# Reciprocals before the broadcast in a two-layer hybrid attention kernel, and the gates' products in smaller portions

## The chip, the core and the metric

The kernel runs on one core of a Trainium2 chip. The core has five engines that run side by side, each through its own instruction stream in order: TensorE (PE in the profile, its weight loads PEld), VectorE (DVE), ScalarE (ACT), GpSimd (POOL) and SyncE (SP), whose stream issues most of the DMAs. They wait for one another by semaphores. The metric is device time in microseconds (us), the median of several executions; less is better.

## What is computed

Two layers of a diffusion trunk over 512 latent tokens and 256 context tokens of width 1024. Each layer normalises its input, projects it once, runs two attention branches over parts of that projection, multiplies each by a SiLU gate, projects them to the model width, merges them by sigmoid gates, projects once more and adds the result, scaled by a residual gate, to the stream. The residual gate is a part of `silu(c) @ w_ada + b_ada`. The second branch is grouped-query attention:

```python
def _attend(q, k, v):
    s = jnp.einsum('bqkgd,btkd->bkgqt', q, k).astype(jnp.float32) * (HEAD_DIM ** -0.5)
    p = jax.nn.softmax(s, axis=-1).astype(v.dtype)
    return jnp.einsum('bkgqt,btkd->bqkgd', p, v)
...
    b_att = _gqa_latent(qb, k_all, v_all)          # 8 query heads, 2 key heads, 768 keys
...
    o_a = (a_att * jax.nn.silu(a_z)) @ w_o_a
    o_b = (b_att * jax.nn.silu(b_z)) @ w_o_b
    merged = jax.nn.sigmoid(g_a) * o_a + jax.nn.sigmoid(g_b) * o_b
    return merged @ w_out
...
    x_new = x + gate_x * out_x
```

In the first layer the context tokens are updated as well, so that they too have queries; in the second they are not.

## The kernel before

**Numbers in two halves.** Large products are made of three matmuls (`mm3`, L421): high half by high half, high by low, low by high. A weight tile of 128x512 comes by an SP DMA into `raw`, ScalarE writes its rounded high half `whi`, and VectorE or GpSimd the rest, `wlo` (`load_w` L385, `load_w2` L400).

**Order.** A planner walks through the program as it is written, with its own costs of each instruction, and places each on its engine's stream when it holds that the inputs are there. What it has placed is fixed: on the chip each engine takes its stream in order. The helper `behind(engine, fn)` (L461) ties what `fn` issues on one engine behind the instruction issued last on that engine. Transposes that are put off (`turn_late`, L473) are tied in this way on TensorE.

**Before grouped-query attention (the projection stage).** In layer 0 the list `bg` (L1085) holds the residual gates' products, 34 steps from `gate_steps((0, 1), ...)`: for each of two halves of the inner dimension one load of the vector `cb` (two DMAs), and then, for 8 tiles and 2 vectors each, one product with its sum over the free dimension (`dot`, L280): L285 on VectorE, tied behind the latest VectorE instruction. The first of the two products of a tile issues the tile's load (`rawb`, L278, on SP); two buffers hold the tiles. In layer 1 `bg` is empty. Six projections of keys and values (`tok_proj`, L1097) run two steps each; then the loop over `qt` token blocks (six in layer 0) makes the queries: a projection of 24 matmuls of 128x512, the squares (ScalarE), their sums (L493, VectorE), the power -0.5 (L496, GpSimd), the scaling (L505) and the rotation (L574, and for latent blocks L576 on GpSimd and L579), all of which end in four transposes (L517) that are put off by two blocks; and then `run(bg, 4)` (L1114) takes four steps from the list. So the 22 steps that are left are all issued by the sixth block. After that come four pieces of filling work (`fill`, L1122; two in layer 1), each a projection of the merge gates, with the transposes that are still put off. Then the pool of this stage is closed (L1125), and the pool of the attention takes over its memory, tile by tile.

**Grouped-query attention.** It runs through 8 units `u` (`pipeline`, L1004): a pair of heads and half of the latent queries each. `gq_first` (L1137) makes four score tiles of 128x768 (L879, L880), a bound of their maximum (L1151, VectorE), the exponentials with their sums over the keys (L1152, ScalarE, sums into `r`, 128x2x2, one column for each of two query blocks and two heads), and two halves in 16 bits (L824 on ScalarE, L825 on VectorE or GpSimd), which a DMA transposes. `gq_second` (L1166) of the unit before follows, and then filling work. In `gq_second` the sums are not divided into the probabilities but into the gate: `divide` (L831) makes reciprocals, each repeated 64 times, as a tile `rb` of 128x256; two transposes on TensorE (L836) turn it into one half of a PSUM tile, and VectorE multiplies it and a factor `back` into the gate (L837). `pair_values` (L839) then multiplies the turned probabilities with the values into the other half of that PSUM tile (L844), and L1179 multiplies both. Layer 0 has a second `divide` for the context queries in every second unit, with the sums `rc`; that makes 8 + 4 divisions in layer 0 and 8 in layer 1.

**Filling work there.** The rest of the merge gates' projections (L612, L616) and the first branch's output projection (high and low halves of its input L658 and L659, products L694), by `run(fill, ...)` after each unit; before the last unit's values, `early` (L1181) issues loads and high and low halves of the second branch's gate.

Of the kernel before, what the change touches and what calls it, by code (L numbers as in the profile page):

```python
# [60 lines left out]
def hybrid_kernel(es: ExitStack, tc, x, ctx, cvec, w_ada, w_ada0, small, gvec, w_in, w_o_a, w_o_b, w_out,  # L61
                  bias_int, bias_edge, rope, ident_d, out):
    nc = tc.nc
    V, S, G, T = nc.vector, nc.scalar, nc.gpsimd, nc.tensor
# [10 lines left out]
    def nm(s):  # L75
        uid[0] += 1
        return f"{s}_{uid[0]}"
# [188 lines left out]
    def ada_steps(l, tiles, halves, nv, pool, queue=None):  # L266

        cb = {}

        def load(h):  # L270
            cb[h] = pool.tile([128, 2, 512], F32, tag="cb", name=nm("cb"), bufs=1)
            for v in range(nv):
                src = cd[8 * v + 4 * h:8 * v + 4 * h + 4].rearrange("k p -> (k p)").unsqueeze(0)
                nc.sync.dma_start(cb[h][:, v, :], src.to_broadcast([128, 512]))

        def load_tile(h, i):
            cb["w"] = pool.tile([128, 512], F32, tag="rawb", name=nm("rawb"), bufs=2)
            (queue or nc.sync).dma_start(cb["w"], w_ada[l, h, i])  # L278

        def dot(h, i, v):  # L280
            if v == 0:
                load_tile(h, i)
            w = cb["w"]
            o = w if v == nv - 1 else pool.tile([128, 512], BF16, tag="junk", name=nm("junk"), bufs=1)
            behind(ON_DVE, lambda: V.tensor_tensor_reduce(o, w, cb[h][:, v, :], 1.0, 0.0, ALU.mult, ALU.add,  # L285
                                                          asum[:, i, h, v:v + 1]))
        res = []
        for h in halves:
            res += [lambda h=h: load(h)] + [lambda h=h, i=i, v=v: dot(h, i, v) for i in tiles for v in range(nv)]
        return res  # L290
# [6 lines left out]
    def ada_mod(l):  # L297
        mod_finish(l, ada_sum(0, 16, 2).rearrange("p (a k) v -> p a k v", a=2), 0, 8)

    def ada_gate(l, nv, pool):  # L300

        g = sp.tile([128, 2, 8], F32, tag="ag", name=nm("ag"), bufs=1)
        n = 8 * nv
        V.tensor_tensor(g[:, 0:nv], ada_sum(16, 24, nv)[:, :, 0:nv].rearrange("p k v -> p v k"),
                        gcol[:, 52 + 8 * l:60 + 8 * l].unsqueeze(1).to_broadcast([128, nv, 8]), ALU.add)
        V.tensor_scalar(g[:, 0:nv], g[:, 0:nv], 0.5, None, ALU.mult)
        pt = psw(512, "t")
        T.transpose(pt[0:n, 0:128], g[:, 0:nv].rearrange("p v k -> p (v k)"), ident)
        gt = pool.tile([16, 128], F32, tag="agt", name=nm("agt"), bufs=1)
        S.copy(gt[0:n], pt[0:n, 0:128])  # L310
        nc.sync.dma_start(gd[l][0:n], gt[0:n])
# [121 lines left out]
    def tok_proj(w, n, a, t, evac):  # L433

        ps = psw(n)
        tok_mm(ps, w, n, a, t, 0, KT)
        evac(t, ps)
        turn_late(hp["lag"])
# [22 lines left out]
    def behind(engine, fn, after=None):  # L461

        n = len(nc.cur_bb.bb.instructions)
        after = latest(engine, 1) if after is None else after
        fn()
        for i in nc.cur_bb.bb.instructions[n:]:
            if i.engine == engine:
                for last in after:
                    tc.add_manual_dep(i, last, mybir.DependencyInfo(
                        mybir.DependencyClass.NoSync, mybir.DependencyReason.DATA), reason="program order")  # L470
                after = [i.name]

    def turn_late(n):  # L473

        while len(hp["late"]) > n:
            behind(ON_PE, hp["late"].pop(0))

    def run(fill, n):
        for _ in range(min(n, len(fill))):
            fill.pop(0)()  # L480
# [102 lines left out]
    def layer(l, hx, nxt, start):  # L583
# [8 lines left out]
        def gate_steps(halves, pool):  # L592
            return ada_steps(l, range(16, 24), halves, nv, pool)
# [104 lines left out]
        if first:  # L698
# [22 lines left out]
            bg = ada_steps(1, range(16), (0,), 2, hp["p"])  # L721
        else:
# [5 lines left out]
            bg = gate_steps((0, 1), hp["p"]) + [lambda: ada_gate(l, nv, hp["p"])]  # L728
# [49 lines left out]
        if True:  # L778
# [52 lines left out]
            def divide(ps, r, dst, back):  # L831

                rb = att["p"].tile([128, 2, 128], F32, tag="rb", name=nm("rb"), bufs=2)
                V.reciprocal(rb.rearrange("p i (e d) -> p i e d", e=2), r.unsqueeze(3).to_broadcast([128, 2, 2, 64]))
                for i in range(2):
                    T.transpose(ps[:, 128 * i:128 * i + 128], rb[:, i, :], ident)  # L836
                V.scalar_tensor_tensor(dst, ps, back, dst, ALU.mult, ALU.mult)  # L837
# [21 lines left out]
            def stage_k(src, e, kh, kl, dup):  # L859

                k = rows(src, e)
                V.tensor_copy(rows(kh, e), k)
                S.copy(rows(kh, 1 - e), k)
                (G if dup else V).tensor_tensor(rows(kl, e), k, F(rows(kh, e)), ALU.subtract)
                if dup:
                    S.copy(rows(kl, 1 - e), F(rows(kl, e)))
# [56 lines left out]
            def open_att(name, width, n_p, n_t, n_h):  # L923
                st = ExitStack()
                att["p"] = st.enter_context(tc.tile_pool(name=name, bufs=2, reuse_waits="tile"))
                att["w"], att["np"], att["nt"], att["nh"] = width, n_p, n_t, n_h
                att["turn"], att["spare"] = 0, False
                return st
# [150 lines left out]
            def split_vb():  # L1079
                size(vf.rearrange("p t n -> p (t n)"), vbig[:, 1152:1920], vbig[:, 2946:2947])  # L1080
                shrink(vbig[:, 2946:2947], vs, vbig[0:1, 2948:2949], 0.5)
                halves(vf.rearrange("p t (h d) -> p (t h) d", h=2), vb.rearrange("p t h q d -> p (t h) q d"),
                       vs[:, 0:1])

            bg = gate_steps((0, 1), hp["p"]) if first else []  # L1085
# [25 lines left out]
                    rope_heads(4, ps, rs, gbc[:, 0, :], None, qbv, t)  # L1111
            for t in range(qt):
                tok_proj(w_q, 512, a_hx, t, evac_bq)
                run(bg, 4)  # L1114
                if t == STAGE_T[0]:
                    split_vb()
                if t in STAGE_T:
                    e = STAGE_T.index(t)
                    stage_k(kbv[:, 0, :], e, gkt[e][0], gkt[e][1], True)

            zb = big("zb")
            for i in range(PRE_GQ * len(spans)):  # L1122
                run(fill, 1)
                turn_late(1 if i == 0 else 0)
            bp_es.close()  # L1125
            gq_es = open_att(f"gq{l}", 768, NP_GQ[l], 0, NH_GQ[l])
            open_ps(s=(2, 1024), v=(1, 512))
# [38 lines left out]
            def gq_second(u, st):  # L1166

                j, b = u // 2, u % 2
                ht, r, cts, rcs = st
                vsl = lambda k, q: vb[:, k, j // 2, q, :]  # L1170
                ps = psw(512, "t")
                work = [(ps, zv[:, j, 256 * b:256 * b + 256], r, vsl, lambda e, a, k: ht[:, :, e, 6 * a + k, :], 6)]
                if b == 1 and first:
                    work.append((psw(512, "v"), zv[:, j, 512:768], rcs, lambda k, q: vsl(4 + k, q),
                                 lambda e, a, k: cts[e][:, a, :, k, :], 2))
                for ps, dst, r, v, pr, n in work:
                    divide(ps[:, 256:512], r, dst, vs[:, 1:2])
                    behind(ON_PE, lambda: pair_values(ps[:, 0:256], v, pr, n), [])
                    V.tensor_tensor(dst, ps[:, 0:256], dst, ALU.mult)  # L1179
# [11 lines left out]
        with tc.tile_pool(name=f"mrg{l}", bufs=1, reuse_waits="tile") as mp:  # L1191
# [34 lines left out]
            bg = ada_steps(1, range(16), (1,), 2, mp, G) + [lambda: ada_mod(1)] if first else []  # L1226
# [205 lines left out]
    def nxt():  # L1432
        if not hx1:
            hx1.extend([[big("hx") for _ in range(2)] for _ in range(2)])
        return hx1
    layer(0, hx0, nxt, start)
    layer(1, hx1, None, None)


# [73 lines left out]
```

## Time and profile before

| what | value |
|---|---|
| median of 3 runs | 1114.02 us (1111.32 to 1115.77) |
| the profiled execution's own time | 1115.85 us |
| its span, first to last instruction | 1114.1 us |
| VectorE busy over the span | 783.1 us |
| ScalarE busy over the span | 607.9 us |
| GpSimd busy over the span | 441.2 us |

The profile is of one execution. Its views group instructions by line and shape, say who waited for whom, list the instructions of an engine in order of time, and sum up the busy time of each engine in a stretch. Matmuls are pipelined, so that TensorE can be busy without being at its peak; the ends of matmuls are modelled. A line of a view names the engine, the line of the kernel, the operation and its output and inputs.

### The profile page before, as it was taken

Reading aid. Unit: us, or ns where it says so; the run is one execution under the profiler, and the core shown is the slowest. Engines: PE = TensorE matmul, PEld = TensorE weight load, DVE = VectorE, ACT = ScalarE, POOL = GpSimd, SP = SyncE. Lnnn points to the kernel's source line nnn. Section 1 sums busy time; section 2 is a strip of 40 time slices with the busy share of each in tenths; the row PEclk is TensorE's granted clock in tenths of the full one; section 3 lists DMA queues with packets and bytes.
Section 4 is the critical chain, followed back from the end, with each engine's and each line's share of the span. In section 5 each row is a group of like instructions: output and inputs, shape, how many; then the busy total and the mean of one; then the engine's idle time right before and its main releaser. Section 6 shows DMA issues by size and latency. Waiting matters only on the chain. (4 is left out here: it accounts for less than half of the span.)

```text
span 1114.1 us, 17673 instructions
## 1 busy us (share of the span) xinstructions
PE 1074.7 (96%) x6032; PEld 883.2 (79%) x6032; DVE 783.1 (70%) x1626; ACT 607.9 (55%) x1236; POOL 441.2 (40%) x375
## 2 busy tenths in 40 slices
PE   8999999899999899988999999999999999999998
PEld 5688888788887778876888778888877888877777
DVE  4667799974388486766576875466997665879573
ACT  6464279776333467665231275444999346676430
POOL 1054235554256143353412444332455472453531
PEclk9999999999999999999999999999999999999999
DMA  9455325555545277789624532453555536889742
GB/s 369 149 169 149 90 70 116 124 137 121 174 121 179 86 177 185 174 219 248 210 76 130 189 120 69 136 170 102 126 145 126 150 113 171 195 236 218 201 151 77
DMA packets 236002, 171.83 MB, mean 154 GB/s; under 512 B 160140, under 2 KB 201864, under 8 KB 234248
## 3 DMA queue, kind: packets, MB, share of 16 engines
q1 hardware_dynamic: 228576, 156.31, 51.6%
q0 software_dynamic: 2368, 7.87, 2.1%
q10 hardware_dynamic: 4968, 6.53, 1.8%
q8 instruction: 47, 0.77, 0.3%
q14 instruction: 43, 0.35, 0.1%
HBM read 115.58 MB, written 17.32 MB: 119 GB/s over the span
## 5 line engine op out<-in xcount | busy, mean ns | idle before, releaser
L825 POOL TENSOR_TENSOR h<-p,h 128x256 f16<-128x256 f32 (+2 forms) x104 | 111.2, 1078 | 199.5 <-ACT h L824 154.2
L410 POOL TENSOR_TENSOR wlo<-raw,whi 128x512 fp32r<-128x512 f32 x70 | 97.7, 1399 | 136.8 <-ACT whi L408 100.5
L423 PE MATMUL psf<-hx,whi 128*128 128x512 f32 (+1 forms) x360 | 137.3, 382 | 1.5 <-DVE zt L614 1.2
L424 PE MATMUL psf<-hx,whi 128*128 128x512 f32 (+1 forms) x360 | 135.7, 377 | 0.0
L425 PE MATMUL psf<-hx,wlo 128*128 128x512 f32 (+1 forms) x360 | 135.3, 376 | 0.0
L408 ACT CAST whi<-raw 128x512 fp32r<-128x512 f32 x136 | 82.9, 620 | 74.0 <-DMA raw<-in_w_in_dram 52.5
L423 PE MATMUL psx<-whi,hx 128*128 128x512 f32 (+1 forms) x328 | 121.7, 373 | 0.0
L424 PE MATMUL psx<-wlo,hx 128*128 128x512 f32 (+1 forms) x328 | 120.1, 367 | 1.3 <-DVE wlo L396 1.3
L425 PE MATMUL psx<-whi,hx 128*128 128x512 f32 (+1 forms) x328 | 120.1, 367 | 0.0
L396 POOL TENSOR_TENSOR wlo<-raw,whi 128x512 fp32r<-128x512 f32 x40 | 59.2, 1483 | 126.5 <-ACT whi L393 83.1
L393 ACT CAST whi<-raw 128x512 fp32r<-128x512 f32 x88 | 54.0, 624 | 94.3 <-PE psx L425 32.1
L496 POOL TENSOR_TENSOR ss<-ss,ehalf 128x8 f32<-128x8 f32 (+2 forms) x40 | 63.6, 1594 | 78.0 <-DVE ss L493 69.6
L824 ACT CAST h<-p 128x256 f16<-128x256 f32 (+2 forms) x136 | 81.2, 617 | 12.3 <-DMA ht<-h 9.3
L1151 DVE CUSTOM_DVE_ANT_0 p<-pss,vb 128x768 f32<-128x768 f32 x64 | 59.9, 949 | 35.1 <-PE pss L880 31.2
L1152 ACT ACTIVATE p<-pss,mx 128x768 f32<-128x768 f32 x64 | 57.5, 901 | 41.0 <-DVE mx L1151 40.6
L423 PEld LDWEIGHTS psf<-hx,whi 128*128 128x128 f32 x360 | 67.8, 188 | 14.7 <-DVE zt L614 1.6
L410 DVE TENSOR_TENSOR wlo<-raw,whi 128x512 fp32r<-128x512 f32 x66 | 60.8, 925 | 26.3 <-ACT whi L408 26.2
L425 PEld LDWEIGHTS psf<-hx,wlo 128*128 128x128 f32 x360 | 67.8, 188 | 11.7
L424 PEld LDWEIGHTS psf<-hx,whi 128*128 128x128 f32 x360 | 67.9, 189 | 11.2 <-issue 0.6
L424 PEld LDWEIGHTS psx<-wlo,hx 128*128 128x128 f32 x328 | 62.0, 189 | 11.6 <-DVE wlo L396 2.4
L425 PEld LDWEIGHTS psx<-whi,hx 128*128 128x128 f32 x328 | 61.9, 189 | 10.5 <-DVE hx L339 0.4
L423 PEld LDWEIGHTS psx<-whi,hx 128*128 128x128 f32 x328 | 61.9, 189 | 9.4 <-issue 0.2
(330 smaller groups left out, 2938.9 us busy)
## 6 DMA issues: line engine op xcount, KB each, us to landing
raw<-in_w_in_dram SPq DMA_DIRECT2D x168, 256.0 KB, 3.0
rawb<-in_w_ada_dram SPq DMA_DIRECT2D x48, 256.0 KB, 2.7
raw<-in_w_out_dram SPq DMA_DIRECT2D x32, 256.0 KB, 2.9
tg<-gs SPq DMA_DIRECT2D x4, 1536.0 KB, 8.4
rawx<-in_w_ada_dram SPq DMA_DIRECT2D x4, 1024.0 KB, 10.2
rawy<-in_w_ada_dram SPq DMA_DIRECT2D x4, 1024.0 KB, 9.9
gs<-zt ACTq DMA_DIRECT2D x16, 256.0 KB, 2.6
raw<-in_w_o_a_dram SPq DMA_DIRECT2D x16, 256.0 KB, 3.7
```

Source lines behind the costliest of these rows:

```text
L393: S.copy(hi[:, :n], raw[:, :n])
L396: e.tensor_tensor(lo[:, :n], raw[:, :n], F(hi[:, :n]), ALU.subtract)
L408: S.copy(hi, raw)
L410: lo_eng(i).tensor_tensor(lo, raw, F(hi), ALU.subtract)
L423: T.matmul(ps, lhs[0], rhs[0], start=first, stop=False)
L424: T.matmul(ps, lhs[0], rhs[1], start=False, stop=False)
L425: T.matmul(ps, lhs[1], rhs[0], start=False, stop=last)
L496: G.tensor_tensor(ss, ss, ehalf[:, :n], ALU.pow)
L824: S.copy(h[:, 0], p[:, :n])
L825: eng.tensor_tensor(h[:, 1], p[:, :n], h[:, 0], ALU.subtract)
L1151: V.tensor_tensor_reduce(p, pss, lift, -1.0, 3e38, ALU.add, ALU.min, mx[:, 0:1])
L1152: S.activation(p, pss, AF.Exp, bias=mx[:, 0:1], accum_out=r[:, i, e:e + 1])
```

## The change

The reciprocal is taken of the sums themselves, in place (128x4), by VectorE; ScalarE then writes each of them 64 times side by side into `rb`. And in the projection stage each block of the query loop takes three steps from `bg`, not four; each of the pieces of filling work after the loop takes one; and whatever is left then is taken before the pool is closed (in layer 0 nothing is: 12 + 18 + 4 = 34).

```diff
             def divide(ps, r, dst, back):
 
                 rb = att["p"].tile([128, 2, 128], F32, tag="rb", name=nm("rb"), bufs=2)
-                V.reciprocal(rb.rearrange("p i (e d) -> p i e d", e=2), r.unsqueeze(3).to_broadcast([128, 2, 2, 64]))
+                V.reciprocal(r, r)
+                S.copy(rb.rearrange("p i (e d) -> p i e d", e=2), r.unsqueeze(3).to_broadcast([128, 2, 2, 64]))
                 for i in range(2):
                     T.transpose(ps[:, 128 * i:128 * i + 128], rb[:, i, :], ident)
                 V.scalar_tensor_tensor(dst, ps, back, dst, ALU.mult, ALU.mult)
...
             for t in range(qt):
                 tok_proj(w_q, 512, a_hx, t, evac_bq)
-                run(bg, 4)
+                run(bg, 3)
                 if t == STAGE_T[0]:
                     split_vb()
...
             for i in range(PRE_GQ * len(spans)):
                 run(fill, 1)
                 turn_late(1 if i == 0 else 0)
+                run(bg, 1)
+            run(bg, len(bg))
             bp_es.close()
             gq_es = open_att(f"gq{l}", 768, NP_GQ[l], 0, NH_GQ[l])
```

## The prediction

> **What bounds the kernel now.** I read the page's first part, then the busy time by stage (own stretches: end of the query projections, attention of layer 0, attention of layer 1).
>
> ```profile
> span 1114.1 us, 17673 instructions
> PE 1074.7 (96%) x6032; PEld 883.2 (79%) x6032; DVE 783.1 (70%) x1626; ACT 607.9 (55%) x1236; POOL 441.2 (40%) x375
> 363.60:380.00 16.40, 13.15 (x66) 11.12 (x65) 6.87 (x19) 6.37 (x13) 1.29 (x1) 0.90 0.20 66
> 380.00:545.00 165.00, 155.17 (x1061) 127.37 (x1060) 115.77 (x192) 99.47 (x202) 67.45 (x46) 0.99 0.83 204
> 925.00:1064.00 139.00, 133.79 (x808) 107.53 (x807) 104.48 (x152) 88.36 (x161) 60.68 (x40) 1.00 0.81 202
> ```
>
> The columns behind the length are busy times of PE, PEld, DVE, ACT and POOL, then the granted clock. TensorE is busy 96% of the span, and in each of the three stretches the change touches. So the change can only win back what TensorE loses there: 16.40 - 13.15 = 3.25 us, 9.8 us and 5.2 us of idling, and time at a lower clock. Who ended that idling, by the waits of PE (the first two rows from the whole run, the next five from 380 to 545, the last three from 925 to 1064; total, times, longest):
>
> ```profile
> PE pst L517 <- DVE rr L574: 3.2, 1, 3.2
> PE pst L517 <- DVE rr L579: 1.0, 1, 1.0
> PE pst L836 <- DVE rb L834: 2.2, 2, 1.4
> PE pst L844 <- DVE zb L837: 1.7, 1, 1.7
> PE psf L423 <- DVE tg L694: 1.5, 4, 0.5
> PE pss L879 <- ACT p L1152: 1.2, 3, 0.7
> PE pss L879 <- ACT p L901: 0.7, 1, 0.7
> PE pss L879 <- ACT p L1152: 2.3, 3, 1.5
> PE psf L423 <- DVE tg L694: 1.2, 3, 0.6
> PE pst L836 <- DVE rb L834: 0.8, 1, 0.8
> ```
>
> Nearly all go back to VectorE, directly or by the exponentials that wait for its maxima. And the clock, around the two longest of these waits:
>
> ```profile
> 363.10:366.50 3.40, 0.90 (x4) 0.38 (x3) 1.91 (x6) 0.38 (x1) 0.00 (x0) 1.00 0.48 161
> 366.50:369.90 3.40, 2.65 (x9) 2.29 (x10) 3.02 (x10) 1.48 (x4) 0.00 (x0) 0.51 0.00 0
> 523.50:526.90 3.40, 1.49 (x7) 1.08 (x8) 3.40 (x9) 3.28 (x8) 1.64 (x2) 1.00 1.25 184
> 526.90:530.30 3.40, 3.40 (x9) 2.21 (x7) 1.97 (x2) 1.68 (x5) 3.37 (x3) 0.51 1.22 273
> ```
>
> After a stretch in which TensorE was busy 0.90 or 1.49 us of 3.40, the next 3.4 us run at half the clock. That loses half of the busy time in it: 2.65 / 2 = 1.3 us and 3.40 / 2 = 1.7 us.
>
> **Part A, the products (layer 0 only).** The fourth step of a block goes to the next, so that the last seven products (of 32) and three of the tile loads are issued later. What they do now stands in the timelines of DVE (first four rows), POOL and PE:
>
> ```profile
> 364.59 0.69 DVE L285 CUSTOM_DVE_ANT_0 junk<-rawb,cb 128x512 bf16<-128x512 f32 x1 [1.68 <-DMA rawb<-in_w_ada_dram]
> 365.21 0.69 DVE L505 TENSOR_TENSOR ry<-psx,ss 128x512 f32<-128x512 f32 x1
> 366.42 0.69 DVE L574 TENSOR_TENSOR rr<-ry,gbc 128x512 f32<-128x512 f32 x1
> 382.12 0.96 DVE L1151 CUSTOM_DVE_ANT_0 p<-pss,vb 128x768 f32<-128x768 f32 x1 [10.16 <-PE pss L880]
> 361.20 1.64 POOL L496 TENSOR_TENSOR ss<-ss,ehalf 128x8 f32<-128x8 f32 x1 [3.73 <-DVE ss L493]
> 367.25 1.08 PE L517 MATMUL pst<-ident,rr 128*128 128x128 f32 x4 [3.25 <-DVE rr L574]
> ```
>
> The last block's scaling L505 could start when GpSimd's power ends, at 361.20 + 1.64 = 362.84. It starts at 365.21, behind a product that waits 1.68 us for its tile; then another product stands between L505 and L574, and TensorE idles 3.25 us. The first five blocks now issue 32 of the 34 steps; after the change 27, and the products that stand in the way here, steps 29 to 32, are then issued after the sixth block and tied behind its L574. So L505 at 362.9 and L574 end at about 364.3: some 0.3 us of the wait stay. Gain 2.95 us; the clock's 1.3 us; and of the 1.0 us wait for L579 of an earlier block, which has products around it in the same numbers, half: 0.5. **A = 4.7 us**; bounds 0 (the planner still puts products or their loads ahead) and 3.25 + 1.3 + 1.0 = 5.6. I take 4.7 since the order is forced by the ties, not left to the planner. The moved loads stay on SP among the same weight loads; VectorE has room for the moved products in the 10.16 us before 382.12, in which it waits for TensorE. That idling is the cover of these products, and of the pool's memory being freed later: if it were gone, four more products of 0.69 us would cost 2.8 us.
>
> **Parts B and C, the reciprocals.** Groups by line and shape, and (last row) how often the exponential's engine sat idle before it until VectorE's maximum:
>
> ```profile
> L834 DVE RECIPROCAL rb<-r 128x256 f32<-128x256 f32 x16 | 28.0, 1748 | 1.0 <-ACT p L1152 0.8
> L834 DVE RECIPROCAL rb<-rc 128x256 f32<-128x256 f32 x4 | 6.9, 1723 | 0.3 <-ACT p L901 0.3
> L781 DVE RECIPROCAL r<-r 128x1 f32<-128x1 f32 x64 | 9.6, 156 | 3.5 <-ACT p L972 2.8
> L824 ACT CAST h<-p 128x256 f16<-128x256 f32 x64 | 24.1, 401 | 2.1 <-DVE p L787 1.0 <-issue 0.5
> L1152 ACT ACTIVATE p<-pss,mx 128x768 f32<-128x768 f32 x64 | 57.5, 901 | 41.0 <-DVE mx L1151 40.6
> L1152 ACT ACTIVATION_READ_ACCUMULATOR p<-pss,mx 128x1 f32 x64 | 12.4, 193 | 0.0
> DVE mx L1151: 40.6, 30
> ```
>
> Removed from VectorE: 28.0 + 6.9 = 34.9 us. Added: 20 reciprocals of 128x4. No row shows this shape; between 156 ns for 1 element and 1748 for 256, the slope is 6.2 ns, so 156 + 3 x 6.2 = 175 ns, 3.5 us in all. VectorE is lighter by 31.4 us. ScalarE gets 20 writes of 128x256 float32 with a repeated input, which no row shows either; below, the cast of that size, 401 ns; above, the 901 ns of three times the size; I take 0.40 us, 8.0 us in all. The way to `rb` is 0.18 + 0.40 us in place of 1.75, so the write may start up to 1.17 us after the reciprocal before `rb` is late. New wait: ScalarE waits for VectorE in each division, and behind it stand exponentials and casts, for which the next scores, the low halves and the transposing DMAs wait.
>
> *B, layer 0.* Tied to L834 directly: 2.2 us (`rb`), 1.7 us (the values of L844 wait for L837, which stands behind two reciprocals in a row) and the clock's 1.7 us: 5.6. Behind VectorE in general: 1.5 + 1.2 + 0.7 = 3.4. I do not take these whole, since ScalarE's stream is full where a write would be wanted. At the wait of 1.4 us:
>
> ```profile
> 522.73 2.30 ACT L658 CAST gbh<-zb 128x768 fp32r<-128x768 f32 x3
> 523.09 1.74 DVE L834 RECIPROCAL rb<-r 128x256 f32<-128x256 f32 x1
> ```
>
> Where the write falls behind these casts, `rb` is there at 525.03 + 0.40, later than the present 524.83; where the planner puts it ahead of them, 1.2 us earlier. Half of the direct part and a quarter of the other: **B = 2.8 + 0.9 = 3.7 us**, bounds 0 and 9.0 (a loss is the third rival).
>
> *C, layer 1.* There 14.0 us of VectorE's 104.48 in 139 go, and the waits behind it are 2.3 + 1.2 + 0.8 = 4.3 us. Half, for the same reason: **C = 2.1 us**, bounds 0 and 4.3.
>
> What is late next: TensorE itself, and then the low halves on GpSimd. Here a rule speaks against the change. Rows first: VectorE, GpSimd, VectorE, GpSimd, and the groups of L825 on VectorE from 380 to 545 and from 925 to 1064:
>
> ```profile
> 1010.50 1.75 DVE L834 RECIPROCAL rb<-r 128x256 f32<-128x256 f32 x1
> 1010.43 1.66 POOL L825 TENSOR_TENSOR h<-p,h 128x768 f16<-128x768 f32 x1 [3.16 <-ACT h L824]
> 1035.58 2.03 DVE L825 TENSOR_TENSOR h<-p,h 128x768 f16<-128x768 f32 x1
> 1035.08 1.72 POOL L410 TENSOR_TENSOR wlo<-raw,whi 128x512 fp32r<-128x512 f32 x1
> L825 DVE TENSOR_TENSOR h<-p,h 128x768 f16<-128x768 f32 x16 | 20.4, 1278 | 13.2 <-ACT h L824 13.2
> L825 DVE TENSOR_TENSOR h<-p,h 128x768 f16<-128x768 f32 x16 | 21.9, 1367 | 5.7 <-ACT h L824 5.7
> ```
>
> The old reciprocal and GpSimd's subtraction run side by side at full speed; two subtractions side by side slow each other, 2.03 us against group means of 1278 and 1367 ns. The Trainium skill, "SBUF — State Buffer", section "Who interferes with whom", says that a VectorE instruction with one SBUF input does not contend with GpSimd and one with two does. By that rule, with which the trace agrees, 35 us of harmless cover for GpSimd go, and more of the subtractions meet; the second rival below prices that from the rows.
>
> **Sum.** 4.7 + 3.7 + 2.1 = 10.5 us. Against the profiled execution's own 1115.85 that gives 1105.35; that execution is 1.83 above the median shown, 1114.02. I take 1105.3 (from the median it would be 1103.5).
>
> **The clock's rule.** The Trainium skill, "TensorE: Matmul & The Clock Gate", section "What's actually happening", has the clock halved after an idle window of about 3.4 us. The trace agrees in the length, but a window with 1.49 us of work was enough at 523.5. By the page's rule alone the second drop would not hang on these waits; without its half, 0.85, the sum would be 9.65.
>
> **The rivals.**
> 1. *All waits behind VectorE go.* For it: its share of the waits. Against it: two products of loads and GpSimd (L659, the transposing DMA) end later waits. 5.6 + 9.0 + 4.3 = 18.9, so 1097.0.
> 2. *Only the products pay; the freed VectorE time is given back.* If the 32 subtractions on VectorE, now 1278 and 1367 ns, all came to 2.03, that takes 16 x 0.75 + 16 x 0.66 = 22.6 of the 31.4 us. B and C are then 0 and 1115.85 - 4.7 = 1111.1. For it: TensorE's waits there are short and many, and the planner arranges them anew. Against it: the 1.7 and 1.4 us waits have a reciprocal just before them.
> 3. *ScalarE becomes late (slower).* The write stands in ScalarE's stream behind an exponential that waits for a maximum: 40.6 us in 30 waits is 1.35, and with 0.90 and 0.19 for reading its sum 2.44 us, 1.27 over the 1.17 allowed. TensorE takes its two transposes in order and stands. Today 3 of 20 show on TensorE. With 4 shown it eats part A; from 9 on the kernel is slower by over 0.5%; with 11, and nothing won in B and C, 14.0 - 4.7 = 9.3: 1125.1. For it: ScalarE idles 41.0 us in front of those exponentials with everything behind them held. Against it: the reciprocal waits for that unit's exponentials, so the planner knows the write late, and 20 short gaps suffice.
> 4. *The parts change nothing that can be seen*: the products' loads end later and hold the first score tiles for the 2.8 us named in A, and the rest comes out even: 1115.85 - 4.7 + 2.8 = 1114.0.
>
> **Chances.** Forecast 0.46; rival 1 0.10; rival 2 0.24; rival 3 0.09; rival 4 0.11. About 0.5% (5.6 us) is what a measurement of this kernel can tell from no change. Faster by more: the forecast and rival 1, 0.56; within: rivals 2 and 4, 0.35; slower: 0.09. The range reaches from 1098, just above rival 1, to 1115.5, past rivals 2 and 4; rival 3 and half of rival 1 are left out.
>
> **What the changed profile would show.** A: no wait of L517 for L574 over 0.5 us and full clock around 366; products last until about 372, inside VectorE's idling before the first L1151. B and C: L834 as 20 reciprocals of about 175 ns, a new ScalarE line of 20 writes of about 0.40 us, waits for L837 and `rb` below 2 us in all, full clock around 527. The forecast is wrong if TensorE waits for the ScalarE line for more than 5 us in all, if L825 on VectorE rises towards 2 us, or if the waits move to GpSimd's L410 and L659.

## The result, and the profile after

The changed kernel takes **1105.5 us** (median, 1104.34 to 1109.23) against 1114.02: ratio 0.9931, 95% interval 0.9913 to 0.9949. Run once more on another chip, beside the experiments below, it came to 0.9955 (0.9939 to 0.9971), so its gain is 5 to 8.5 us. The profiled execution took 1109.23 us, 3.7 above its median, and its span fell from 1114.1 to 1107.5 us. The forecast of 1105.3 was right as a number, partly by luck: it took 10.5 us off a profiled execution that lay 1.8 us above the median, while the gain is 8.5 us at most. Its parts were not all right, and two effects that it did not have cancel each other; this is the subject of what follows.

First the profile page after, its first part (busy time and share of the span by engine):

```profile
span 1107.5 us, 17679 instructions
PE 1070.9 (97%) x6032; PEld 885.3 (80%) x6032; DVE 753.8 (68%) x1626; ACT 613.4 (55%) x1256; POOL 437.8 (40%) x375
```

VectorE fell by 29.3 us; ScalarE rose by 5.5, less than the 8.0 of its 20 writes. TensorE's busy time fell by 3.8 us though it does the same matmuls. The clock is not the reason: it is halved for 13.7 us in this trace (8.9 to 12.3, 357.0 to 360.4 and 647.2 to 654.0) and for 10.2 us before (8.1 to 11.5, 366.5 to 369.9 and 527.0 to 530.4). Part B below comes back to this. Now the two new lines (duration ns min/median/max, first and last start):

```profile
L834 DVE RECIPROCAL r<-r x16: 168/174/178, 390.9 to 1029.2; 128x4 f32<-128x4 f32 x16
L834 DVE RECIPROCAL rc<-rc x4: 166/170/178, 414.8 to 518.2; 128x4 f32<-128x4 f32 x4
L835 ACT COPY rb<-r x16: 396/404/417, 391.3 to 1029.5; 128x256 f32<-128x256 f32 x16
L835 ACT COPY rb<-rc x4: 398/402/415, 415.1 to 520.9; 128x256 f32<-128x256 f32 x4
```

Both prices are those of the prediction, 175 ns and 0.40 us. The stage rows that answer to the three of before (busy PE, PEld, DVE, ACT, POOL, then the clock; the attentions end sooner, so their stretches are shorter):

```profile
363.60:380.00 16.40, 16.40 (x98) 14.54 (x97) 9.15 (x27) 6.42 (x16) 2.43 (x2) 1.00 0.37 117
379.00:537.00 158.00, 147.84 (x1041) 124.03 (x1039) 99.31 (x190) 102.46 (x213) 68.19 (x45) 1.00 0.83 208
925.00:1058.00 133.00, 128.24 (x789) 103.59 (x789) 89.48 (x155) 90.68 (x168) 59.80 (x39) 1.00 0.85 208
```

The stretch from 363.6 us, where TensorE lost 3.25 us and clock, is full. But in the attention of layer 0 it still idles 158.00 - 147.84 = 10.2 us, no less than the 9.8 of before. These waits of TensorE in the whole run bear on the change (us in total, times, longest; lines from L835 on stand one further down than in the kernel before, the later ones three). Another, for the exponentials L1155, is as large as before: 3.5 us against 3.4.

```profile
PE psf L423 <- DVE tg L694: 3.3, 4, 1.7
PE pst L845 <- DVE zb L838: 2.6, 2, 1.4
PE psv L837 <- ACT rb L835: 2.2, 1, 2.2
PE pst L517 <- DVE rr L579: 1.9, 1, 1.9
PE pst L331 <- ACT half L334: 1.8, 2, 1.0
```

The wait for `rb` has become one wait of 2.2 us, that for `zb` rose from 1.7 to 2.6, that for L579 from 1.0 to 1.9, and a wait for the normalization's `half` (0.6 before) is at 1.8. The clock fell in this execution behind the wait for L579 (and again at 647 us, in the merge):

```profile
352.80:356.30 3.50, 1.57 (x9) 1.03 (x8) 2.64 (x3) 0.00 (x0) 3.48 (x3) 1.00 0.02 7
356.30:359.90 3.60, 3.60 (x14) 2.83 (x12) 3.60 (x8) 1.59 (x3) 2.54 (x2) 0.60 0.63 197
```

**Where the time went, by stretches.** Stages overlap, so equal times are poor landmarks. Instead I add up the matmuls of each trace in order of time, each with the usual time of its shape from start to start (0.23 us for 128x512 float32), and compare the times at which two traces have done the same sum. In the kernel before, the borders lie at 341, 387, 610, 694, 940 and 1060 us. A border serves only where all traces have the same order of matmuls around it: from 1051 to 1053 us the kernel before does the values of the last unit, which others do sooner, and a border there would move up to 0.8 us between attention 1 and the tail. The table has what each trace gained (-) or lost (+) against the trace of before within a stretch, in us; the kernels are those of the experiments.

| trace | to 341 | end of query projections | attention 0 | merge 0, normalization | to 940 | attention 1 | tail | span |
|---|---|---|---|---|---|---|---|---|
| changed | +0.8 | -2.2 | -3.7 | +2.1 | +0.3 | -1.9 | -2.0 | -6.6 |
| after_again | +1.1 | -2.4 | -3.9 | +1.9 | -0.2 | -2.2 | -2.0 | -7.7 |
| e1_products | -1.5 | -2.7 | +0.4 | +0.2 | -0.7 | -1.1 | 0.0 | -5.4 |
| e2_reciprocals | -1.5 | +0.5 | -3.8 | +1.3 | -0.1 | -3.7 | -2.0 | -9.3 |
| e3_load_back | +0.3 | -2.1 | -4.8 | +1.7 | -1.6 | +2.8 | -2.0 | -5.7 |
| e4_copy_vector | 0.0 | -2.6 | -2.9 | -0.4 | -1.6 | -1.1 | -2.0 | -10.5 |
| e6_copy_gpsimd | +0.2 | -2.5 | +0.1 | +0.1 | -1.3 | +0.2 | -2.0 | -5.1 |
| e7_more_buffers | -0.1 | -2.5 | -0.5 | -4.7 | -1.2 | -2.6 | -2.0 | -13.5 |
| e8_before_buffers | -1.1 | +1.9 | -0.4 | -4.7 | -1.2 | -1.1 | 0.0 | -6.6 |
| e9_vector_buffers | -1.5 | -2.6 | -0.4 | -4.7 | -1.3 | -0.5 | -2.0 | -13.0 |
| e10_products_later | +0.3 | -5.8 | -1.5 | +2.9 | -0.7 | -3.0 | -2.0 | -9.6 |
| e11_all | 0.0 | -5.6 | +2.8 | -4.7 | -1.6 | -1.1 | -2.0 | -12.2 |
| e12_both | -1.0 | -5.7 | +1.6 | -4.7 | -0.8 | -2.3 | -2.0 | -14.9 |

The first column is chance: up to 341 us nothing differs, and it ranges over 2.6 us. In the second, e8_before_buffers has the work of before and yet +1.9 (its clock is halved for 6.8 us there, from 365.5, in place of 3.4). These are single executions; the verdicts are the ratios of the timed runs.

### The profile page after: what moved, and what is told of

It reads as the page before. It is cut to its first block, busy times and chain, and to the rows that moved or that the text cites. A ratio compares the mean times of both kernels' runs of the same rounds, so it can differ in the third digit from the quotient of the medians.

```text
span 1107.5 us, 17679 instructions
## 1 busy us (share of the span) xinstructions
PE 1070.9 (97%) x6032; PEld 885.3 (80%) x6032; DVE 753.8 (68%) x1626; ACT 613.4 (55%) x1256; POOL 437.8 (40%) x375
## 5 line engine op out<-in xcount | busy, mean ns | idle before, releaser
L825 POOL TENSOR_TENSOR h<-p,h 128x256 f16<-128x256 f32 (+2 forms) x104 | 114.0, 1104 | 193.5 <-ACT h L824 150.9
L410 POOL TENSOR_TENSOR wlo<-raw,whi 128x512 fp32r<-128x512 f32 x70 | 96.7, 1385 | 138.5 <-ACT whi L408 123.5
L396 POOL TENSOR_TENSOR wlo<-raw,whi 128x512 fp32r<-128x512 f32 x40 | 55.9, 1401 | 132.8 <-ACT whi L393 97.2
L496 POOL TENSOR_TENSOR ss<-ss,ehalf 128x8 f32<-128x8 f32 (+2 forms) x40 | 64.6, 1616 | 78.2 <-DVE ss L493 73.4
L824 ACT CAST h<-p 128x256 f16<-128x256 f32 (+2 forms) x136 | 81.5, 617 | 12.3 <-DMA ht<-h 6.9
L410 DVE TENSOR_TENSOR wlo<-raw,whi 128x512 fp32r<-128x512 f32 x66 | 65.2, 990 | 32.8 <-ACT whi L408 32.5
L1154 DVE CUSTOM_DVE_ANT_0 p<-pss,vb 128x768 f32<-128x768 f32 x64 | 60.1, 952 | 34.4 <-PE pss L881 30.9
L1155 ACT ACTIVATE p<-pss,mx 128x768 f32<-128x768 f32 x64 | 57.4, 899 | 25.9 <-DVE mx L1154 25.5
```

The lines of the kernel that those rows point to most:

```text
L396: e.tensor_tensor(lo[:, :n], raw[:, :n], F(hi[:, :n]), ALU.subtract)
L410: lo_eng(i).tensor_tensor(lo, raw, F(hi), ALU.subtract)
L496: G.tensor_tensor(ss, ss, ehalf[:, :n], ALU.pow)
L824: S.copy(h[:, 0], p[:, :n])
L825: eng.tensor_tensor(h[:, 1], p[:, :n], h[:, 0], ALU.subtract)
L1154: V.tensor_tensor_reduce(p, pss, lift, -1.0, 3e38, ALU.add, ALU.min, mx[:, 0:1])
```

## The experiments

**Each part alone, and the whole again.** The first kernel has the products' spread on top of the kernel before, the second the reciprocals:

```diff
-                run(bg, 4)
+                run(bg, 3)
...
+                run(bg, 1)
+            run(bg, len(bg))
```

> Only the products' spread (three steps a block and the rest behind the last block); the reciprocals as before. Theory of the two parts (each wins by its own waits): 2.2 us (what the trace of after shows of it up to 360 us, where it has a new wait of 1.93 us for L579 and the halved clock behind it) to 4.7 us (the prediction's part A), so a ratio of 0.9958 to 0.998, and the wait of L517 for L574 under 0.5 us. Rival, the gain is given back behind it: the wait for L574 is gone, but a later stage loses the same, ratio 0.9995 or above. Second rival, the whole gain hangs on it: ratio at 0.994 or below.

```diff
-                V.reciprocal(rb.rearrange("p i (e d) -> p i e d", e=2), r.unsqueeze(3).to_broadcast([128, 2, 2, 64]))
+                V.reciprocal(r, r)
+                S.copy(rb.rearrange("p i (e d) -> p i e d", e=2), r.unsqueeze(3).to_broadcast([128, 2, 2, 64]))
```

> Only the reciprocals (128x4 on VectorE, written out by ScalarE); four products a block as before. Theory of the two parts: 3.8 us in layer 0's grouped attention, 1.0 us in layer 1's, and up to 2.5 us behind the attentions, so 4.8 to 7.3 us, a ratio of 0.9935 to 0.9957; the wait of L517 for L574 stays at about 3.2 us with the halved clock behind it; with the products' 2.2 to 4.7 us it makes up the 8.5 us of the whole change. Rival, the gains do not add up (the planner's other order, not the waits, makes them): this one has either nearly all of it (0.994 or below, with the products at 0.999) or less than 2 us (0.998 or above).

> The changed kernel once more, beside the parts on the same chip: ratio 0.991 to 0.995. If the halved clock at 647 to 654 us belongs to the change (its order of work), this trace has it again and merge and normalization after layer 0's attention take about 2.7 us longer than before; if it is chance of one execution, it is gone here, and the profiled time comes to 1105 to 1106.

The products alone: 0.9972 (0.9954 to 0.9990), 3.1 us. The reciprocals alone: 0.9966 (0.9949 to 0.9983), 3.8 us, less than the 4.8 to 7.3 expected. The product of the two is 0.9938; the whole gave 0.9931 and 0.9955. So the parts add up within their intervals, and the rival in which the whole gain hangs on one of them falls. In e2_reciprocals the wait of L517 for L574 is there as before (3.7 us). In after_again the clock is halved again behind the merge's wait (649.2 to 652.6), so that this belongs to the change.

Of the wait for L574, 1.5 us are left in e1_products, where less than 0.5 was expected. What the products leave is seen in the waits of TensorE in e1_products between 336 and 375 us, and in the clock around them (windows, columns as above):

```profile
PE pst L517 <- DVE rr L574: 1.5, 1, 1.5
PE pst L517 <- DVE rr L579: 1.4, 1, 1.4
```

```profile
350.60:354.00 3.40, 2.02 (x12) 1.44 (x11) 2.67 (x4) 0.00 (x0) 3.40 (x3) 1.00 0.07 14
354.00:357.40 3.40, 3.40 (x17) 2.78 (x16) 3.37 (x7) 1.59 (x3) 2.06 (x2) 1.00 0.80 216
360.80:364.20 3.40, 1.90 (x16) 1.69 (x15) 2.46 (x7) 0.46 (x2) 1.06 (x1) 1.00 0.58 191
```

Before, these two waits were 3.2 and 1.0 us with the halved clock (1.3 us) behind the first: 5.5. Now 2.9 and no lower clock: 2.6 won, the 2.7 of the table. In the changed kernel's first trace the wait for L574 is gone, but only because TensorE was itself late there: the wait for L579 was 1.9 and the 3.6 us behind it ran at 0.60, which loses 3.60 x 0.40 = 1.4. That is 3.3 against 5.5, the 2.2 of the table. Why 1.5 us are left of L574, the timelines of VectorE and GpSimd in e1_products show:

```profile
357.87 0.68 DVE L410 TENSOR_TENSOR wlo<-raw,whi 128x512 fp32r<-128x512 f32 x1
358.47 0.68 DVE L285 CUSTOM_DVE_ANT_0 junk<-rawb,cb 128x512 bf16<-128x512 f32 x1
359.08 0.69 DVE L493 TENSOR_REDUCE ss<-sq 128x8 f32<-128x520 f32 x1
...
361.90 0.69 DVE L505 TENSOR_TENSOR ry<-psx,ss 128x512 f32<-128x512 f32 x1 [0.91 <-POOL ss L496]
362.62 0.69 DVE L574 TENSOR_TENSOR rr<-ry,gbc 128x512 f32<-128x512 f32 x1
...
359.92 1.95 POOL L496 TENSOR_TENSOR ss<-ss,ehalf 128x8 f32<-128x8 f32 x1 [3.85 <-DVE ss L493]
```

L505 now starts when GpSimd's power L496 ends, as forecast. But the chain L493, L496, L505, L574 begins no sooner than before: ScalarE's squares are there at 356.44, and the first link, L493, starts at 359.08, behind a low half and a product. Measured from 341 us on, where e1_products is 1.5 us ahead, L493 starts 0.2 us later than before, and L496 takes 1.95 us in place of 1.64. TensorE, on the other hand, comes sooner: the planner has put 2006 matmuls ahead of these transposes, 2010 before, which is some 0.9 us. Whether fewer products help was tested with e10_products_later, below.

On the clock here: the windows with 2.02 and 1.90 us of work in 3.40 were followed by the full clock, those with 0.90, 1.49 and 1.57 (of 3.50) by the halved one. The windows are placed by me around the waits, so these are no threshold.

**VectorE's freed time, or the short way to `rb`?** In the changed kernel a reciprocal of the old shape is put back, into a tile that nobody reads:

```diff
+                rj = att["p"].tile([128, 2, 128], BF16, tag="rj", name=nm("rj"), bufs=1)
...
+                    V.reciprocal(rj.rearrange("p i (e d) -> p i e d", e=2), r.unsqueeze(3).to_broadcast([128, 2, 2, 64]))
```

> The changed kernel with a reciprocal of 128x256 into a tile that nobody reads, behind each write of ScalarE: VectorE has its 34.9 us again, while the way to rb stays short (0.17 + 0.40 us). Theory of the short way: what counts is how soon rb is there, so most of the gain stays, 1 to 2 us over the changed kernel (ratio to before 0.994 to 0.995). Rival, the freed time of VectorE counts (the waits for zb, for the maxima and for L694): the reciprocals' 4.8 to 7.3 us go, ratio 0.997 to 0.999, and the waits of PE for zb L838 and for p L1155 come to more than 5 us in layer 0's grouped attention.

Measured: 0.9942 (0.9924 to 0.9961), no slower than the changed kernel on the same chip (0.9955). With VectorE as full as before, attention 0 gained 4.8 us against 3.9. So VectorE's busy time was not what bounded that attention. In attention 1 this trace lost 2.8 us, where after_again won 2.2. Its clock is halved there from 992.5 to 995.9 and from 1033.5 to 1040.3, which costs some 4.7 us, half of TensorE's busy time in them; whether VectorE's load brought that about, as the rival has it, one trace does not settle.

**The write on another engine.** In the changed kernel the copy goes to VectorE, or to GpSimd:

```diff
-                S.copy(rb.rearrange("p i (e d) -> p i e d", e=2), r.unsqueeze(3).to_broadcast([128, 2, 2, 64]))
+                V.tensor_copy(rb.rearrange("p i (e d) -> p i e d", e=2), r.unsqueeze(3).to_broadcast([128, 2, 2, 64]))
```

> The changed kernel with the write of the 128x256 copy on VectorE, behind the reciprocal, in place of ScalarE: VectorE gets about 20 x 0.41 = 8 us of its freed time back, ScalarE is as before, and no write stands behind an exponential. Theory of the short way (what counts is how soon rb is there): 0.17 + 0.41 us, the same way, so the gain stays, ratio 0.992 to 0.9955, and the wait of PE for rb of 2.1 to 2.4 us in one place goes, since that one is ScalarE's queue. Rival, ScalarE's queue holds rb in many places and hides a better result: ratio at 0.991 or below.

> The changed kernel with that copy on GpSimd: VectorE stays freed, ScalarE is as before, but the way to rb is long again (0.17 us and a copy of some 0.75 us, half of a 128x512 subtraction of 1.39 us, often behind a subtraction of 1.4 to 1.7 us). Theory of the short way: half of the reciprocals' gain or more goes, ratio 0.996 to 0.9995, and PE waits for rb more than 3 us in all. Rival, VectorE's freed time makes the gain: it stays, ratio 0.993 to 0.9955.

VectorE: 0.9925 (0.9904 to 0.9945). GpSimd: 0.9946 (0.9927 to 0.9966), faster than I expected, and my premise was wrong. The group of GpSimd's copies in e6:

```profile
L835 POOL COPY rb<-r 128x256 f32<-128x256 f32 x16 | 6.9, 432 | 60.1 <-DVE r L834 50.6 <-ACT h L824 8.2 <-DMA raw<-in_w_o_a_dram 1.3
```

GpSimd writes it in 0.43 us, not 0.75, so its way to `rb` is no longer than ScalarE's, and this run cannot tell a long way from a short one. It shows something else: the 60.1 us behind the bar are GpSimd standing in front of its copies, 50.6 of them for the reciprocal, with its subtractions L825 and L410 queued behind. No wait of TensorE for `rb` is left there, and still attention 0 gains nothing (+0.1 in the table). Its clock is halved there for 6.8 us, from 493.3, and its waits are others:

```profile
PE pst L845 <- DVE zb L838: 2.4, 3, 1.4
PE psf L423 <- ACT zt L612: 2.4, 2, 1.6
PE pss L880 <- ACT p L1155: 2.3, 2, 2.0
PE psv L845 <- DMA vb<-h: 2.1, 1, 2.1
```

So **taking away the waits for `rb` is not by itself a gain** in this stage: other waits take their place.

ScalarE's one wait of 2.2 us in the changed kernel is the third rival's mechanism, in its timelines (VectorE, ScalarE, TensorE):

```profile
518.20 0.17 DVE L834 RECIPROCAL rc<-rc 128x4 f32<-128x4 f32 x1
...
518.49 0.83 ACT L824 CAST h<-p 128x768 f16<-128x768 f32 x1 [1.57 <-DMA ht<-h]
519.71 0.62 ACT L824 CAST h<-p 128x512 f16<-128x512 f32 x1 [0.39 <-DMA ht<-h]
520.42 0.62 ACT L408 CAST whi<-raw 128x512 fp32r<-128x512 f32 x1
520.94 0.40 ACT L835 COPY rb<-rc 128x256 f32<-128x256 f32 x1
...
521.39 0.44 PE L837 MATMUL psv<-ident,rb 128*128 128x128 f32 x2 [2.23 <-ACT rb L835]
```

The sum is inverted at 518.37, but the write stands behind three casts and two waits for a transposing DMA, and ends at 521.3: 3.1 us after the reciprocal's start, against 1.75 of the old way. It costs 2.2 us once in 20.

**The merge behind attention 0.** All traces with the write on ScalarE and two tiles lose 1.3 to 2.9 us there, which nothing in the prediction foresaw. In after_again (timelines of VectorE, ScalarE and TensorE, then windows with the clock):

```profile
641.34 0.69 DVE L285 CUSTOM_DVE_ANT_0 junk<-rawb,cb 128x512 bf16<-128x512 f32 x1 [0.96 <-DMA rawb<-in_w_ada_dram]
642.07 0.69 DVE L285 CUSTOM_DVE_ANT_0 rawb<-rawb,cb 128x512 f32<-128x512 f32 x1
...
643.33 0.17 DVE L230 TENSOR_TENSOR modc<-modc,g 128x16 f32<-128x16 f32 x1
...
643.60 2.91 ACT L334 ACTIVATE half<-pst,modc 128x128 f32<-128x128 f32 x8 [2.57 <-PE psx L425]
...
645.16 0.65 PE L331 MATMUL pst<-ident,y 128*128 128x128 f32 x4 [1.56 <-ACT half L334]
```

```profile
643.00:646.40 3.40, 1.25 (x7) 0.59 (x5) 2.85 (x7) 2.80 (x9) 0.00 (x0) 1.00 0.00 0
646.40:649.80 3.40, 1.92 (x8) 1.38 (x9) 3.22 (x4) 3.40 (x9) 2.62 (x3) 0.91 0.00 0
649.80:653.20 3.40, 3.06 (x12) 1.97 (x10) 3.33 (x5) 3.40 (x10) 2.04 (x2) 0.59 0.62 170
```

Here other products run, those of layer 1's modulation (L285 too, with their loads issued by GpSimd). They wait for their loads, two tiles in turn. When the last is done, the modulation `modc` follows at 643.33, and only then can ScalarE write `half`. TensorE's transposes wait for it, and the clock falls. I had first taken TensorE to be simply too early here. The test gives these loads four tiles:

```diff
-            cb["w"] = pool.tile([128, 512], F32, tag="rawb", name=nm("rawb"), bufs=2)
+            cb["w"] = pool.tile([128, 512], F32, tag="rawb", name=nm("rawb"), bufs=4 if queue else 2)
```

> The changed kernel with four tiles in place of two for the loads of layer 1's modulation products in the merge after layer 0 (line 278, only where GpSimd issues them). Theory of the give-back: in the three traces with the new reciprocals TensorE comes to the normalization's transposes at 643 us, 4.6 us sooner than before, and stands there for the modulation (L230 at 643.3), whose products wait for their loads; with more tiles these end sooner, the waits for half L334 (1.8 to 2.3 us) fall below 1 us, the clock stays full at 647 to 653, and the kernel is 2 to 4 us faster than the changed one: ratio 0.9905 to 0.9925. Rival, the loads' issue on GpSimd or the normalization itself is the bound, or other work is late there: ratio as that of the changed kernel, 0.993 to 0.9955, and the clock still falls.

> The kernel before, with the same four tiles. Theory of the give-back: the modulation is no bound there as long as the attention is late (TensorE lost 1.0 + 0.8 + 0.6 us around 650, no lower clock), so 0 to 1 us: ratio 0.999 to 1.000. Rival, the tiles help whatever the reciprocals do: 2 to 4 us here too, 0.9965 to 0.998.

On the changed kernel: **0.9883** (0.9864 to 0.9902); in its trace the wait for `half` is gone, and no other above the view's bound stands in the merge. On the kernel before: 0.9971 (0.9956 to 0.9986), so half of my theory falls. The tiles win 4.7 us in this stretch whatever the reciprocals do: the modulation was a bound already, spread over several waits (`half` 0.6, the low halves 1.5 in three, `y` 0.4, together 2.5 of the 4.7; the rest is in no wait that the view shows). The other half, "too early", falls with e4_copy_vector: attention 0 ends as early there (0.0 - 2.6 - 2.9 = -5.5 us at the border, against 1.1 - 2.4 - 3.9 = -5.2 in after_again), and the merge loses nothing (-0.4). What differs is the order: in the traces with the give-back 3579 matmuls stand ahead of the transposes of the first tile (3575 in e3 and e10) and 3643 ahead of those of the next; in before, e1, e4 and e6 it is 3595 and 3630. So the give-back goes with a new order of the planner, which it makes for the write on ScalarE with two tiles.

**Combinations, and the products once more.** e9_vector_buffers has the write on VectorE and the four tiles. e10_products_later is the changed kernel with two products a block; e11_all is e9 with this edit, e12_both the changed kernel with it and the four tiles:

```diff
-                run(bg, 3)
+                run(bg, 2)
```

> The write on VectorE (as in e4_copy_vector) together with the four tiles for the modulation's loads. Since the write on VectorE left the merge in the order of the kernel before (no give-back there), the theory that the give-back is the planner's order has the tiles win here what they won in the kernel before, 3.3 to 4.7 us, and not the 6.6 of the changed kernel: from 0.9925 to 0.988 to 0.9895. Rival, the parts share the same gain: 0.991 or above.

> The changed kernel with two products a block in place of three, so that more of them come behind the blocks. Theory of part A: what is left of its waits (L517 for L579, 1.5 to 1.9 us, and for L574, 1.5 us) stands behind products, loads and the low halves that VectorE does in between (L493 of the last block starts at 361.93 behind two of them); with fewer products they fall to 1.0 and 0.5 us, so 1 to 1.5 us less up to 370 us. Rival, the waits are GpSimd's chain (L493, L496, L505) and the collision of L579 with GpSimd: they stay within 0.3 us each. The whole time may also move by the new order behind (2.5 us either way in the merge), ratio 0.990 to 0.9965.

> All three: two products a block, the write on VectorE, four tiles. Theory of separate gains: that of e9_vector_buffers less 0 to 1.5 us, ratio 0.987 to 0.9895. Rival, the planner's other order gives back what the parts win: 0.991 or above.

> The changed kernel (write on ScalarE) with two products a block and with the four tiles. Theory that the gains belong to their places: up to 370 us 5 to 6 us less than before (as in e10_products_later), and in the stretch of the merge no stall, 3.5 to 4.7 us less than before over the same TensorE work in place of 2.3 more; together a ratio of 0.985 to 0.989, at or below that of e7_more_buffers, 0.9883. Rival, the order behind gives back what the products win (as e10_products_later lost 4 us again at 450 to 500 us of TensorE work): 0.990 or above.

| kernel | median us | ratio (95%) |
|---|---|---|
| e9_vector_buffers | 1107.07 | 0.9919 (0.9894 to 0.9944) |
| e10_products_later | 1105.49 | 0.9908 (0.9885 to 0.9931) |
| e11_all | 1103.17 | 0.9881 (0.9859 to 0.9904) |
| e12_both | 1101.07 | 0.9869 (0.9842 to 0.9897) |

e9 has the 4.7 us of the tiles in its trace, but its timed runs went from 1102.84 to 1110.74, and it cannot be told from e4 (0.9925); of its two theories none is settled. e10 settles part A: between 336 and 375 us its trace has no wait of TensorE above the view's bound, neither for L574 nor for L579, and the stretch gains 5.8 us. It is not the queue just ahead of the last L493 that became shorter, as VectorE's timeline shows; a product and a low half still stand there, in the other order (the product at 356.50):

```profile
357.11 0.68 DVE L410 TENSOR_TENSOR wlo<-raw,whi 128x512 fp32r<-128x512 f32 x1
357.71 0.68 DVE L493 TENSOR_REDUCE ss<-sq 128x8 f32<-128x520 f32 x1
358.32 0.67 DVE L285 CUSTOM_DVE_ANT_0 rawb<-rawb,cb 128x512 f32<-128x512 f32 x1
```

The squares are there at 354.85, and L493 starts 2.9 us behind them, as late as in e1_products (2.6). What came sooner is the chain's beginning: of the traces, e10_products_later is 1.8 us behind e1_products at 341 us, and yet its L579 starts at 349.68 against 351.33 and its last squares at 354.26 against 355.85, that is 3.4 us sooner. The TensorE work is at the same place for L574 (2006 matmuls ahead in both), and GpSimd's part did not change (L496 takes 1.95 us in both, L579 beside it 1.77 and 1.75). So the number of products in the blocks before was the cause and not GpSimd's chain; I had expected 1 to 1.5 us of this run and got 3.4 more than the changed kernel in that stretch. Part of it went again in attention 0 (-1.5 in place of -3.9). e11 and e12 came out where separate gains would put them, yet not without a give-back: attention 0 lost 2.8 us in e11, with one wait of 5.5 us for a transposing DMA, and 1.6 in e12. e12_both is the fastest measured, **1101.07 us**; its interval does not meet that of the changed kernel, but overlaps those of e7 and e11. Against after_again its trace has 3.3 us from the products and 6.6 from the tiles, and 5.5 given back in attention 0.

## Why the prediction was right as a number, and where it was not

**The shapes and prices** were right: 20 reciprocals of 0.17 us, 20 writes of 0.40 us, VectorE lighter by 29 us.

**Part A, 4.7 us forecast, 2.2 to 2.7 measured.** The mechanism was right: L505 no longer stands behind a product that waits for its load. The failing step is "L505 at 362.9 and L574 end at about 364.3: some 0.3 us of the wait stay", and the half of the wait for L579. I took GpSimd's end and TensorE's arrival as fixed and looked only at the products between L505 and L574. In e1 the chain ends some 0.5 us later than that (L493 by 0.2, L496 by 0.3), and TensorE comes to the transposes some 0.9 us sooner, by the planner's order. So 1.5 us stayed of L574's wait where it shows, and L579's wait grew by 0.4 to 1.0, again with the transposes four matmuls sooner. L579's own duration also grew, from 0.68 to 1.75 us in e1, beside GpSimd; e10 has that too and no wait. That the changed kernel's first trace shows the forecast sign, no wait for L574 and the full clock at 366 us, is chance, since after_again has the 1.5 us. With two products a block the stretch reached 5.8, just past the upper bound of 5.6.

**Part B, 3.7 forecast, 3.7 to 3.9 measured, but not through the waits that it was built on.** The text expected the waits for L837 and `rb` (now L838 and L835) below 2 us in all; they are 2.6 and 2.4, against 1.7 and 2.2. The same TensorE work in both kernels (kernel before, then changed):

```profile
386.90:610.20 223.30, 213.47 (x1354) 177.08 (x1353) 156.38 (x276) 109.44 (x222) 78.32 (x56) 0.99 0.69 177
```

```profile
385.50:605.10 219.60, 209.39 (x1354) 176.74 (x1353) 138.96 (x264) 114.83 (x237) 80.88 (x55) 1.00 0.68 179
```

TensorE's idling is 9.83 and 10.21 us: nothing was won there. The 3.7 us are in its busy time, 213.47 - 209.39 = 4.1. Of these 1.7 are the halved clock at 527 us. It is gone as forecast in both traces of the changed kernel, but not for good: each of the nine other kernels with the new reciprocals has one or two halved stretches again between 484 and 542 us (e3, with the largest gain, from 501.0 to 504.4). The rest, 2.4, lies in pauses too short for the records to show them as idle, since the end of one matmul covers the start of the next: by the starts alone, pauses over 0.5 us come to 10.1 us before and 10.6 in after_again, those of 0.06 to 0.5 us (the halved clock's among them) to 13.8 and 9.5. That the sum agrees with 2.8 + 0.9 is thus partly luck. What makes it is not settled: it outlives VectorE's load (e3), it goes with the write on GpSimd, and with the four tiles, which only change the order behind and around it, 0.5 of it is left (e7). e2 has the same gain with the clock halved again. Over the ten kernels with the new reciprocals this stretch runs from -4.8 to +2.8, and over the three with the old ones from -0.4 to +0.4. So the planner's order has a share in it that these runs cannot separate from the reciprocals'.

**Part C, 2.1 forecast, some 1 us measured.** The changed kernel shows -1.9 and -2.2, but e1 and e8, which have the old reciprocals, show -1.1 as well: the one execution of before was slow there. With the write on another engine (e4, e6, e9, e11) nothing is left beyond these 1.1 us; with it on ScalarE the other traces have -2.3 to -3.7, but for e3. The waits that the text named did fall by about half, from 4.3 to 1.9 us, but others came (changed kernel, 922 to 1058 us):

```profile
PE pst L845 <- DMA ht<-h: 2.5, 3, 1.1
PE pss L880 <- ACT p L1155: 1.5, 2, 1.4
PE psf L423 <- DVE tg L694: 0.4, 1, 0.4
```

The first of these, for the transposing DMA, is not among the waits of before in this stretch. The step that failed is to count half of the named waits as won: what stands behind them was not priced.

**Two terms were missing.** The merge gives back 2 us, with the planner's new order. The tail wins 2.0 us in every trace with the new reciprocals, wherever the write is done, and in none of the three with the old ones. Most of it is one wait: between 1050 us and the end, the kernel before has

```profile
PE psf L424 <- POOL wlo L396: 1.7, 1, 1.7
```

and after_again no wait at all. VectorE's load is not it, since e3 has the gain too; why GpSimd's low half is in time there is not shown. What I did not weigh for either: an edit in one helper lets the planner arrange everything behind it anew, hundreds of microseconds on. The number came out because +2 and -2.0 cancel, and because the base, 1.8 us above the median, made up for most of what A and C lack. From the median the same sum gives 1103.5, 2.0 below the measured one.

**The rivals.** The first (all waits go) did not happen, and the fourth (nothing to be seen) falls by the interval, which ends at 0.9949. The second priced the freed VectorE time as spent in subtractions slowed by GpSimd; L825 on VectorE became faster instead (from 380 and 925 us it was 1278 and 1367 ns):

```profile
L825 DVE TENSOR_TENSOR h<-p,h 128x768 f16<-128x768 f32 x32 | 33.5, 1047 | 16.9 <-ACT h L824 16.6
```

By the rule of the Trainium skill ("SBUF — State Buffer", "Who interferes with whom"), that one SBUF input does not contend with GpSimd and two do, the text expected a loss of cover; this row shows no loss from it. The third (ScalarE late) happened once in 20, for 2.2 us, where it needed nine. In the clock's rule of the Trainium skill ("TensorE: Matmul & The Clock Gate", "What's actually happening") the halving follows an idle window; here it also followed windows with 0.90 to 1.57 us of work, so a window need not be idle throughout. Windows with 1.90 and 2.02 were followed by the full clock, but in the merge one with 1.92 was followed by 0.59, so that windows placed by hand give no limit. Other traces give none either: 1.52 us of work in e1_products (860.5 to 863.9) was followed by the full clock, 1.85 in e10_products_later (517.4 to 520.8) by the halved one.

## What to carry to other kernels

A wait that is named in the profile is worth its length only if nothing else ends just behind it: look for the whole chain ahead of the waiting instruction (here back to the block before), not only for what stands next to it, and ask whether the waiting engine itself will come sooner. Where a planner orders the program, a local edit moves work far behind it; compare the times at which TensorE has done equal work, stretch by stretch, and run each part alone, before a sum that fits is taken for an understanding. A stall that a search for the cause uncovers elsewhere may be the cheapest gain of all, as the two more tiles were here.

## What the runs showed of the hardware that was not expected

The same copy of 128x256 float32 with a repeated input takes 0.40 us on ScalarE and 0.43 on GpSimd, though a subtraction of two inputs of 128x512 takes GpSimd 1.39 us. On VectorE it takes 0.29, but up to 1.55 (e4_copy_vector):

```profile
L835 DVE COPY rb<-r x16: 293/294/1546, 389.9 to 1025.7; 128x256 f32<-128x256 f32 x16
```

```profile
948.75 1.55 DVE L835 COPY rb<-r 128x256 f32<-128x256 f32 x1
948.39 1.76 POOL L825 TENSOR_TENSOR h<-p,h 128x768 f16<-128x768 f32 x1 [3.42 <-issue]
```

The copy ends at 950.30, 0.15 us after GpSimd's subtraction that began before it. Of the 20 copies, all six of 0.55 us and more begin while such a subtraction runs and end 0.15 us after it; they overlap a subtraction of GpSimd by over 0.4 us, and none of the others does by more than 0.15. The Trainium skill ("SBUF — State Buffer", "Who interferes with whom") lists copies among the operations that can block against GpSimd, whoever comes first; this trace agrees, and the old reciprocal, with 1.69 to 1.75 us in all 20 places, shows nothing of it.
